# MoE slots of two expert pairs laid out by token block, one full-row scatter per two pairs, slot gates summed by one-column matmuls

## The chip, the cores and the metric

The kernel runs on one core of one Trainium2 chip. The metric is the device time of one execution in microseconds (us). PE is TensorE's matmul side, PEld its weight loads, DVE is VectorE, ACT is ScalarE, POOL is GpSimd, and SP is the engine whose queue issues the weight transfers. A line number such as L894 is a line of the kernel before. In the profile an fp32 matmul counts as two instructions (two passes), each with its own weight load; so 16 `mm` calls of the code are 32 matmuls of the trace.

## The reference

A trunk of two layers over 256 tokens of width 1024. Each layer has a token mixer (dilated attention in layer 0, a gated MLP in layer 1) and then a mixture of experts; every sub-layer is normed, modulated by a conditioning vector (adaLN) and added to x with a gate `gt`. The change touches the mixture of experts alone:

```python
def hierarchical_moe(h, w_group, b_group, w_expert, b_expert, w_gate, w_up, w_down):
    ...
    # gate: (256 tokens, 16 experts), two experts of one group of four are not zero for a token
    hg = jnp.einsum('td,edf->tef', ht, w_gate)     # 1024 -> 256
    hu = jnp.einsum('td,edf->tef', ht, w_up)
    act = (jax.nn.silu(hg) * hu * gate[..., None]).astype(h.dtype)
    y = jnp.einsum('tef,efd->td', act, w_down)     # 256 -> 1024
    return y.reshape(B, S, D)
    ...
        x = x + (gt_f[:, None, :] * y).astype(x.dtype)
```

## The kernel before, in words

The program is `attention()`, `experts(0)`, `gating()`, `experts(1)`. Each engine runs its instructions in the order in which the code writes them (the schedule is written by hand); DMAs are issued from SP's queue in that order as well. Buffers come from pools: 18 of 1 MB for weights and large tiles (`big`), 8 of half a MB (`mid`), 8 small ones, and in PSUM four single banks (`bank`) and two double ones, which hold the output sums `y[0]` and `y[1]` of the two token blocks of 128 tokens.

In `experts(l)` the router picks two experts for each token and ranks the tokens of each expert inside each block. Each expert has 32 slots (`CAP`) per block, 64 (`SL`) in all. `sel` is the one-hot matrix of tokens to slots. `gather` (L878) multiplies it with the high and low parts of the normed x and leaves the slots' inputs, transposed, in `xeT`; the first half of the experts is gathered ahead of the loop, the second half in pairs 0 to 3.

The loop runs over eight pairs p of two experts. On PE one pair is, in order:

- gate-up (L894): for eight chunks of the 1024 inputs and two experts, 64 slots as columns of PE by 512 weights (256 gate, 256 up) into the bank `pgu`. The two experts are two tiles of 64 columns side by side;
- the branch `extra(p)` (L949 to L977): an overflow pass for slots beyond the 64, which runs for one pair of this input, in layer 1, pair 4;
- two transposes `pst` in `slots` (L900) for the next pair. Their input is the one-hot times the gate (`weigh`, on POOL). ACT copies the result with a running sum, which gives each slot's gate `gs`, and DVE compares it with 0, which gives the one-hot `ST` of slots to tokens;
- in pairs 0 to 3 a piece of `gather`;
- scatter (L945) of the previous pair's result into block 0: `y[0]` gets `ST` times the high part `yhi` and times the low part `ylo`, two halves of 512 columns each, so four matmuls;
- two transposes `pat` (L916) of the activation silu(gate) x up x gs, which ACT (L909) and DVE (L910) make; DVE copies them to `atT` (L918);
- scatter of the previous pair into block 1, four matmuls more;
- down (L927): two halves of 512 outputs, each two chunks by two experts, into the bank `pd`. Then DVE multiplies with `gt` (`yw`, L931), ACT takes the high part (`yhi`, L933) and DVE the low one (`ylo`, L935).

The slots of a pair are 128 rows: expert by block by 32. Half of the rows of `ST` belong to the other block in each scatter. The last pair's result is scattered behind the loop (L1051 to L1054); there the second half of 512 columns goes as one fp32 matmul of `yw` and is not split. Behind it follow layer 1's `gating()` or the final norm and `store`. The sums `y` also take x itself, by identity matmuls (`fill`, L785).

## Time and profile before

| | |
|---|---|
| time, median of 3 runs | 616.01 us (615.84 to 616.3) |
| the profiled execution | 615.77 us, its span 614.0 us |
| PE busy | 570.5 us (93%) |
| weight loads (PEld) | 353.9 us (58%) |
| DVE busy | 346.6 us (56%) |
| ACT busy | 211.9 us (35%) |
| POOL busy | 17.7 us (3%) |
| DMA | 321 GB/s mean, 195.08 MB read |

How to read it: PE is busy in 93% of the span, and the loads run beside the matmuls. That is a mean over stages; what ends the waits in the expert loops is read from the order of time on PE in those loops. The views in order of time have these columns: start in us, duration in us, engine, line, operation, out<-in, tile, shapes and types, count, and in brackets the idle time before it and what ended it. Layer 0's expert loop runs from about 178 to 295 us of the span, layer 1's from 473 to about 597.

### The profile page before, as it was taken

What the parts mean: (1) busy time and instruction counts of PE and PEld (TensorE: products, weight loads), DVE (VectorE), ACT (ScalarE), POOL (GpSimd) and SP (SyncE); (2) the same over time, 40 slices, a digit from 0 to 9 for tenths busy, and PEclk for the clock granted to TensorE, in tenths of its full rate; (3) what the DMA queues carried; (4) which work ended last, traced back from release to release, by engine and by line L of the source; (5) the groups of instructions that cost most, each with busy time, mean ns of one, the idle gap of its engine ahead of it and who ended that gap; (6) DMA issues with size and microseconds to landing.
All of it is one profiled execution on the core that took longest, in us unless ns stands there. A gap on an engine that the chain in (4) does not pass through costs nothing. (4 is left out here: it accounts for less than half of the span.)

```text
span 614.0 us, 8150 instructions
## 1 busy us (share of the span) xinstructions
PE 570.5 (93%) x3010; PEld 353.9 (58%) x3010; DVE 346.6 (56%) x668; ACT 211.9 (35%) x357; POOL 17.7 (3%) x56
## 2 busy tenths in 40 slices
PE   6998999999988999999899989999998999989994
PEld 4766874566443444344577789998875344453341
DVE  3998876452742333232789999899457333323223
ACT  6334345551432211111543754454435111112112
POOL 1000000000010000000000010000001000000000
PEclk9999999999997999999999999999999999999998
DMA  8999869999845899999999638678832799946911
GB/s 330 423 418 420 352 257 375 417 368 420 344 184 214 331 421 420 418 415 421 418 422 395 277 140 294 250 304 350 318 138 86 301 392 416 416 176 251 414 60 68
DMA packets 29188, 197.01 MB, mean 321 GB/s; under 512 B 3328, under 2 KB 3968, under 8 KB 7616
## 3 DMA queue, kind: packets, MB, share of 16 engines
q1 hardware_dynamic: 28832, 195.61, 79.8%
q8 instruction: 38, 0.62, 0.4%
q10 hardware_dynamic: 288, 0.52, 0.2%
q14 instruction: 30, 0.25, 0.1%
HBM read 195.08 MB, written 1.05 MB: 319 GB/s over the span
## 5 line engine op out<-in xcount | busy, mean ns | idle before, releaser
L894 PE MATMUL pgu<-wgu,xeT 128*64 128x512 f32 x512 | 112.7, 592 | 0.0
L894 PEld LDWEIGHTS pgu<-wgu,xeT 128*64 128x64 f32 x512 | 36.6, 137 | 72.3 <-issue 72.0
L219 DVE SCALAR_TENSOR_TENSOR wada<-wada,cact 128x1024 f32<-128x1024 f32 x56 | 66.1, 1217 | 0.7 <-ACT cact L168 0.7
L927 PE MATMUL pd<-wdn,atT 128*64 128x512 f32 x256 | 60.2, 613 | 1.7 <-DVE atT L918 1.7
L933 ACT ACTIVATE yhi<-yw 128x512 fp32r<-128x512 f32 x32 | 20.1, 629 | 94.5 <-DVE yw L931 94.5
L910 DVE SCALAR_TENSOR_TENSOR silu<-pgu,gs,silu 128x256 f32<-128x256 f32 x16 | 7.7, 484 | 75.5 <-ACT silu L909 75.5
L931 DVE TENSOR_TENSOR yw<-pd,gt 128x512 f32<-128x512 f32 x32 | 22.0, 688 | 41.4 <-PE pd L927 41.4
L714 PE MATMUL pu<-hhi,wlo 128*128 128x256 f32 x128 | 37.0, 289 | 2.3 <-DVE wlo L296 2.3
L927 PEld LDWEIGHTS pd<-wdn,atT 128*64 128x64 f32 x256 | 17.4, 140 | 36.1 <-issue 29.1
L714 PE MATMUL pu<-hhi,whi 128*128 128x256 f32 x128 | 37.9, 296 | 0.0
L714 PE MATMUL pu<-hlo,whi 128*128 128x256 f32 x128 | 36.9, 288 | 0.0
L935 DVE TENSOR_TENSOR ylo<-yw,yhi 128x512 fp32r<-128x512 f32 x30 | 20.8, 692 | 21.5 <-ACT yhi L933 13.9
L909 ACT ACTIVATE silu<-pgu 128x256 f32<-128x256 f32 x16 | 6.1, 384 | 74.4 <-PE pgu L894 72.4
L296 DVE TENSOR_TENSOR wlo<-win,whi 128x1024 fp32r<-128x1024 f32 x25 | 30.1, 1219 | 0.6 <-ACT whi L295 0.5
L714 PEld LDWEIGHTS pu<-hhi,wlo 128*128 128x128 f32 x128 | 25.2, 197 | 2.6 <-DVE wlo L296 2.5
L286 ACT ACTIVATE hhi<-hj,B 128x256 fp32r<-128x256 f32 x16 | 8.1, 509 | 53.2 <-DVE hj L280 26.9
L295 ACT ACTIVATE whi<-win 128x1024 fp32r<-128x1024 f32 x25 | 25.7, 1052 | 1.1 <-PE pu L714 1.1
L714 PEld LDWEIGHTS pu<-hlo,whi 128*128 128x128 f32 x128 | 25.3, 198 | 0.0
L714 PEld LDWEIGHTS pu<-hhi,whi 128*128 128x128 f32 x128 | 25.2, 197 | 0.0
L296 DVE TENSOR_TENSOR wlo<-bwo,whi 128x1024 fp32r<-128x1024 f32 x16 | 19.4, 1220 | 7.8 <-ACT whi L295 6.5
L945 PE MATMUL y<-yhi,ST 128*128 128x512 f32 x60 | 21.4, 430 | 0.6 <-PEq L951 0.3
L201 PE MATMUL pada<-wada,cz 128*32 128x512 f32 x160 | 20.7, 603 | 1.3 <-ACT VV L512 1.3
(262 smaller groups left out, 1058.5 us busy)
## 6 DMA issues: line engine op xcount, KB each, us to landing
wgu<-e_gu SPq DMA_DIRECT2D x64, 1024.0 KB, 9.7
wada<-w_ada SPq DMA_DIRECT2D x48, 1024.0 KB, 11.4
wdn<-e_dn SPq DMA_DIRECT2D x32, 1024.0 KB, 10.1
win<-w_in SPq DMA_DIRECT2D x16, 1024.0 KB, 13.3
bwo<-b_wo SPq DMA_DIRECT2D x8, 1024.0 KB, 5.0
wqk<-w_qk SPq DMA_DIRECT2D x8, 960.0 KB, 19.3
wv<-w_v SPq DMA_DIRECT2D x4, 960.0 KB, 19.5
wo<-w_o SPq DMA_DIRECT2D x3, 1024.0 KB, 7.3
```

The source lines that it names most:

```text
L201: mm(acc[l][q * 32:(q + 1) * 32, :], cz[:, k, e:e + 32], w[:, q * 512:(q + 1) * 512], start=(i == i0), stop=(i == i1), skip_group_check=True)
L219: V.scalar_tensor_tensor(w[:, h * D:(h + 1) * D], w[:, h * D:(h + 1) * D], 1.0, cact, op0=OP.mult, op1=OP.mult, accum_out=modc[l][:, c:c + 1])
L286: S.activation(hx[0][:, j, :], t, AF.Identity, bias=bb[:, j:j + 1])
L295: S.activation(hi[:m, :n], w, AF.Copy)
L296: V.tensor_tensor(lo[:m, :n], w, hi[:m, :n].bitcast(F32), op=OP.subtract)
L714: mm(pu[f // 2][:, f % 2, :], w_[:, k * 512 + f * P:k * 512 + (f + 1) * P], x_[:, kc, :], start=(kc == 0 and u == 0 and f % 2 == 0), stop= ...
L894: mm(t[e * SL:(e + 1) * SL, 0:n], x(k, e), WTS[l, p][e, k // 4][:, c:c + n], start=(k == 0), stop=(k == 7), skip_group_check=True)
L927: mm(t[e * SL:(e + 1) * SL, :], at[:, f, e * SL:(e + 1) * SL], WTS[l, p][2, e][:, f, n * 512:(n + 1) * 512], start=(f == 0), stop=(f == 1) ...
L931: V.tensor_tensor(w[:, sl], t, gt[l, 1][:, sl], op=OP.mult)
L933: S.activation(hi[:, sl], w[:, sl], AF.Copy)
L935: V.tensor_tensor(lo[:, sl], w[:, sl], hi[:, sl].bitcast(F32), op=OP.subtract)
L945: mm(y[b][:, n * 512:(n + 1) * 512], st[:, b * P:(b + 1) * P], Y[xi][:, n * 512:(n + 1) * 512], start=(first and xi == 0), stop=(last and ...
```

## The change

Two pairs now form a group r. The slots of pair 2r and 2r+1 are laid out by token block: the 128 rows of one operand are four experts by 32 slots of block 0, those of the other four experts by 32 slots of block 1. Half of each comes from the one pair and half from the other, so that the results of both pairs together make full rows for one scatter per block.

- `gate_up_pair` and `down_pair` replace gate-up and down: the same columns in all, but in four tiles of 32 columns (two experts by two blocks) in place of two tiles of 64, with twice as many instructions.
- The scatter runs once per group and block: in pair 2 for both blocks, in pairs 4 and 6 for block 0 and in pairs 5 and 7 for block 1, with the last group behind the loop as before. In pairs 4 to 7 it stands ahead of `pat`.
- `group` replaces `slots`: two transposes for two pairs, ahead of the loop and in pairs 1, 3 and 5. The slots' gates are summed by four fp32 matmuls of one column with a column of ones (`onef`); DVE copies the sums (`gs2`) out, and ACT's copy with a sum goes.
- ACT's high parts and DVE's low parts are cut into two halves of 64 rows, since the two blocks go to different buffers; in the last pair the second product is cut too, and its order on DVE changes.
- `ada(A_E[l][p])` goes; it issued nothing, since the table `A_E` is all zeros.
- `extra` uses X[0], X[1] and one shared buffer `yx` in place of four buffers of the pool.

The diff, cut:

```diff
+    onef = const.tile([P, 1], F32, name="onef")
+    G.memset(onef, 1.0)
     zeros = const.tile([P, 1], BF16, name="zeros")
     G.memset(zeros, 0.0)
-    sg = [const.tile([P, NB, 2, SL], F32, name=f"sg{i}") for i in range(2)]
-    for t in sg:
-        G.memset(t, 0.0)
+    sg = [const.tile([P, NB, 4, CAP], F32, name=f"sg{i}") for i in range(2)]
...
-        def weigh(p):
-            t = sg[p % 2]
-            es = slice(2 * p, 2 * p + 2)
-            for b in range(NB):
-                G.tensor_tensor(t[:, b, :, b * CAP:(b + 1) * CAP], sel[:, b, es, :].bitcast(F32),
-                                gf[:, b, es, None].to_broadcast([P, 2, CAP]), op=OP.mult)
+        def weigh(r):
+            t = sg[r % 2]
+            for b, i, e, n in ((0, 0, 4 * r, 4), (1, 2, 4 * r, 2), (1, 0, 4 * r + 2, 2)):
+                G.tensor_tensor(t[:, b, i:i + n, :], sel[:, b, e:e + n, :].bitcast(F32),
+                                gf[:, b, e:e + n, None].to_broadcast([P, n, CAP]), op=OP.mult)
...
+        def group(src):
+            t = bank("pst", (P, T + 2))
+            for b in range(NB):
+                nc.tensor.transpose(t[:, b * P:(b + 1) * P], src[:, b].rearrange("p e c -> p (e c)"), ident)
+            for o in range(2):
+                for h in range(2):
+                    mm(t[h * SL:(h + 1) * SL, T + o:T + o + 1],
+                       src[:, h ^ o, 2 * h:2 * h + 2, :].rearrange("p e c -> p (e c)"), onef, start=True, stop=True,
+                       skip_group_check=True)
+            st = small("ST", dt=F32R)
+            V.tensor_scalar(st, t[:, 0:T], 0.0, None, op0=OP.is_gt)
+            gs = sm.tile([P, 2], F32, name="gs2", bufs=3)
+            V.tensor_copy(gs, t[:, T:T + 2])
+            return [gs[:, o:o + 1] for o in range(2)], st
+
+        def gate_up_pair(p, t):
+            for k in range(DC):
+                for q in range(4):
+                    e, b = q % 2, (q // 2) ^ (p % 2)
+                    c = (k % 4) * 512
+                    mm(t[q * CAP:(q + 1) * CAP, :],
+                       xeT[p // 4, k // 4][:, k % 4, 2 * (p % 4) + e, b * CAP:(b + 1) * CAP],
+                       WTS[l, p][e, k // 4][:, c:c + 512], start=(k == 0), stop=(k == 7), skip_group_check=True)
+
+        def down_pair(p, at, Y):
+            w = mid("yw") if p < 6 else Y[2]
+            for n in range(2):
+                t = bank("pd")
+                for f in range(2):
+                    for q in range(4):
+                        mm(t[q * CAP:(q + 1) * CAP, :], at[:, f, q * CAP:(q + 1) * CAP],
+                           WTS[l, p][2, q % 2][:, f, n * 512:(n + 1) * 512], start=(f == 0), stop=(f == 1),
+                           skip_group_check=True)
+                sl = slice(n * 512, (n + 1) * 512)
+                if p < 6 or n == 0:
+                    V.tensor_tensor(w[:, 0:512] if p > 5 else w[:, sl], t, gt[l, 1][:, sl], op=OP.mult)
+                for h in range(2):
+                    rs_, b = slice(h * SL, (h + 1) * SL), h ^ (p % 2)
+                    if p > 5 and n:
+                        V.tensor_tensor(Y[3][rs_, b, :], t[rs_, :], gt[l, 1][rs_, sl], op=OP.mult)
+                        continue
+                    S.activation(Y[0][b][rs_, sl], w[rs_, sl], AF.Copy)
+                    V.tensor_tensor(Y[1][b][rs_, sl], w[rs_, sl], Y[0][b][rs_, sl].bitcast(F32), op=OP.subtract)
+
+        def outputs(p):
+            if p < 6:
+                return [[mid(n, dt=F32R) for b in range(NB)] for n in ("yhi", "ylo")]
+            hi, lo, w = mid("yhi", (P, NB, 512), F32R), mid("ylo", (P, NB, 512), F32R), mid("yw", (P, NB, 512))
+            return [[hi[:, b, :] for b in range(NB)], [lo[:, b, :] for b in range(NB)], mid("yw0", (P, 512)), w]
+
...
-        def down(p, at, ts=(None, None), Y=None, last=False):
-            hi, lo, w = Y or (mid("yhi", dt=F32R), mid("ylo", dt=F32R), mid("yw"))
-            for n in range(2):
-                t = bank("pd") if ts[n] is None else ts[n]
-                for f in range(2):
-                    for e in range(2):
-                        mm(t[e * SL:(e + 1) * SL, :], at[:, f, e * SL:(e + 1) * SL],
-                           WTS[l, p][2, e][:, f, n * 512:(n + 1) * 512], start=(f == 0), stop=(f == 1),
-                           skip_group_check=True)
-                sl = slice(n * 512, (n + 1) * 512)
-                V.tensor_tensor(w[:, sl], t, gt[l, 1][:, sl], op=OP.mult)
-                if not last or n == 0:
-                    S.activation(hi[:, sl], w[:, sl], AF.Copy)
-                if not last:
-                    V.tensor_tensor(lo[:, sl], w[:, sl], hi[:, sl].bitcast(F32), op=OP.subtract)
-            if last:
-                sl = slice(0, 512)
-                V.tensor_tensor(lo[:, sl], w[:, sl], hi[:, sl].bitcast(F32), op=OP.subtract)
-            return hi, lo, w
-
-        def scatter(st, Y, first, last, bs=(0, 1), ns=(0, 1)):
+        def scatter(st, Y, bs=(0, 1), ns=(0, 1)):
             for b in bs:
                 for xi in range(2):
                     for n in ns:
                         mm(y[b][:, n * 512:(n + 1) * 512], st[:, b * P:(b + 1) * P],
-                           Y[xi][:, n * 512:(n + 1) * 512], start=(first and xi == 0),
-                           stop=(last and xi == 1), skip_group_check=True)
+                           Y[xi][b][:, n * 512:(n + 1) * 512], start=False, stop=False, skip_group_check=True)
 
...
-                    xr = mid("xr")
+                    xr = X[0]
...
-                    Y = mid("yhi", dt=F32R), mid("ylo", dt=F32R), mid("yw")
-                    xe = Y[2].rearrange("p (d s) -> p d s", d=DC)
+                    w = X[1]
+                    xe = w.rearrange("p (d s) -> p d s", d=DC)
...
+                    yx = mid("yx", (P, 2, 512), F32R)
+                    for n in range(2):
+                        sl = slice(n * 512, (n + 1) * 512)
+                        V.tensor_tensor(w[:, sl], tx[2 * n], gt[l, 1][:, sl], op=OP.mult)
+                        S.activation(yx[:, 0, :], w[:, sl], AF.Copy)
+                        V.tensor_tensor(yx[:, 1, :], w[:, sl], yx[:, 0, :].bitcast(F32), op=OP.subtract)
+                        for b in range(NB):
+                            for i in range(2):
+                                mm(y[b][:, sl], st[:, b * P:(b + 1) * P], yx[:, i, :], start=False, stop=False,
+                                   skip_group_check=True)
...
-        nxt = slots(weigh(0))
-        sgn = weigh(1)
+        grp = {0: group(weigh(0))}
         ada(A_B[l][3])
-        prev = None
+        Y = {}
         for p in range(8):
-            gs_, st = nxt
+            r = p // 2
             pgu[p] = bank("pgu")
-            gate_up(p, [pgu[p]], lambda k, e: xeT[p // 4, k // 4][:, k % 4, 2 * (p % 4) + e, :])
+            gate_up_pair(p, pgu[p])
...
-            act = activate(pgu[p][:, 0:T], pgu[p][:, T:2 * T], gs_)
-            if p + 1 < 8:
-                nxt = slots(sgn)
-                if p + 2 < 8:
-                    sgn = weigh(p + 2)
+            act = activate(pgu[p][:, 0:T], pgu[p][:, T:2 * T], grp[r][0][p % 2])
+            if r < 3:
+                if p % 2:
+                    grp[r + 1] = group(sgn)
+                else:
+                    sgn = weigh(r + 1)
             if p < 4:
                 gather(1, 2 * p, 2 * p + 2)
-            ada(A_E[l][p])
-            if prev:
-                scatter(*prev, False, False, (0,))
+            if p == 2 or p > 3:
+                scatter(grp[r - 1][1], Y[r - 1], (p % 2,))
             at = turn(act)
-            if prev:
-                scatter(*prev, False, False, (1,))
-            prev = (st, down(p, at, last=p == 7))
+            if p == 2:
+                scatter(grp[r - 1][1], Y[r - 1], (1,))
+            if p % 2 == 0:
+                Y[r] = outputs(p)
+            down_pair(p, at, Y[r])
...
-        st, Y = prev
+        st, Y = grp[3][1], Y[3]
         for b in range(NB):
             s = st[:, b * P:(b + 1) * P]
-            mm(y[b][:, 0:512], s, Y[0][:, 0:512], start=False, stop=False, skip_group_check=True)
-            mm(y[b][:, 512:D], s.bitcast(F32), Y[2][:, 512:D], start=False, stop=True,
-               skip_group_check=True)
-            mm(y[b][:, 0:512], s, Y[1][:, 0:512], start=False, stop=True, skip_group_check=True)
+            mm(y[b][:, 0:512], s, Y[0][b], start=False, stop=False, skip_group_check=True)
+            mm(y[b][:, 512:D], s.bitcast(F32), Y[3][:, b, :], start=False, stop=True, skip_group_check=True)
+            mm(y[b][:, 0:512], s, Y[1][b], start=False, stop=True, skip_group_check=True)
```

The order on PE in layer 0, pair 4, behind the branch of the overflow pass; `pst` are slot transposes, `y_1409` and `y_1410` the sums of token blocks 0 and 1, `pat` the transposed activations, `pd` down. Before:

```order
L900 MATMUL pst_2602<-cst_80,sg1_99 128x128 x2
L945 MATMUL y_1409<-yhi_2416,ST_2166 128x512 x2
L945 MATMUL y_1409<-ylo_2417,ST_2166 128x512 x2
L916 MATMUL pat_2615<-cst_80,silu_2599 128x128 x2
L945 MATMUL y_1410<-yhi_2416,ST_2166 128x512 x2
L945 MATMUL y_1410<-ylo_2417,ST_2166 128x512 x2
```

After:

```order
L974 MATMUL y_1409<-yhi_2244,ST_1985 128x512 x2
L974 MATMUL y_1409<-ylo_2246,ST_1985 128x512 x2
L965 MATMUL pat_2701<-cst_80,silu_2691 128x128 x2
L936 MATMUL pd_2711<-wdn_2310,atT_2704 32x512
L936 MATMUL pd_2711<-wdn_2312,atT_2704 32x512
```

The slot transposes and the scatter behind `pat` are gone; down, now in tiles of 32 columns, follows `pat` directly.

The order on PE in layer 0, pair 5, at the same place. Before:

```order
L900 MATMUL pst_2810<-cst_80,sg0_98 128x128 x2
L945 MATMUL y_1409<-yhi_2624,ST_2387 128x512 x2
L945 MATMUL y_1409<-ylo_2625,ST_2387 128x512 x2
L916 MATMUL pat_2823<-cst_80,silu_2807 128x128 x2
L945 MATMUL y_1410<-yhi_2624,ST_2387 128x512 x2
L945 MATMUL y_1410<-ylo_2625,ST_2387 128x512 x2
```

After:

```order
L909 MATMUL pst_2919<-cst_80,sg1_101 128x128 x2
L912 MATMUL pst_2919<-onef_96,sg1_101 64x1 x4
L974 MATMUL y_1410<-yhi_2245,ST_1985 128x512 x2
L974 MATMUL y_1410<-ylo_2247,ST_1985 128x512 x2
L965 MATMUL pat_2934<-cst_80,silu_2916 128x128 x2
L936 MATMUL pd_2940<-wdn_2547,atT_2937 32x512
```

The four one-column matmuls have come in behind the slot transposes, block 1's scatter has moved ahead of `pat`, and block 0's is not in this pair.

The order on DVE at the end of layer 0's loop; `yw` and `yw0` are products of down with the gate, `ylo` low parts, and `wlo` is the first weight split of the next stage. Before:

```order
L918 COPY atT_3211<-pat_3208 128x256
L931 TENSOR_TENSOR yw_3219<-pd_3220,gt_1569 128x512
L931 TENSOR_TENSOR yw_3219<-pd_3227,gt_1569 128x512
L938 TENSOR_TENSOR ylo_3218<-yw_3219,yhi_3217 128x512
L296 TENSOR_TENSOR wlo_3239<-win_3234,whi_3238 128x1024
```

After:

```order
L967 COPY atT_3353<-pat_3350 128x256
L941 TENSOR_TENSOR yw0_3152<-pd_3355,gt_1588 128x512
L948 TENSOR_TENSOR ylo_3150<-yw0_3152,yhi_3149 64x512 x2
L945 TENSOR_TENSOR yw_3151<-pd_3369,gt_1588 64x512 x2
L296 TENSOR_TENSOR wlo_3385<-win_3380,whi_3384 128x1024
```

The second product has moved behind the low parts, and both are cut in two.

## Rows read from the trace of the kernel before

**Rows 1.** PE in order of time, layer 0, pair 4; columns above, with the profile.

```profile
240.95 7.04 PE L894 MATMUL pgu<-wgu,xeT 128*64 128x512 f32 x32
248.30 0.41 PE L900 MATMUL pst<-cst,sg 128*128 128x128 f32 x2 [0.31 <-PEq L951]
248.46 0.71 PE L945 MATMUL y<-yhi,ST 128*128 128x512 f32 x2
...
249.48 0.38 PE L916 MATMUL pat<-cst,silu 128*128 128x128 f32 x2
...
250.72 3.65 PE L927 MATMUL pd<-wdn,atT 128*64 128x512 f32 x16
```

**Rows 2.** What ended the idle time before L894, whole run (us, times).

```profile
  DMA wdn<-e_dn: 0.3, 1
```

**Rows 3.** PE in order of time, layer 1, pairs 0 and 1.

```profile
473.03 0.41 PE L900 MATMUL pst<-cst,sg 128*128 128x128 f32 x2
...
481.96 0.38 PE L916 MATMUL pat<-cst,silu 128*128 128x128 f32 x2
483.30 3.65 PE L927 MATMUL pd<-wdn,atT 128*64 128x512 f32 x16 [0.96 <-DVE atT L918]
...
495.33 0.63 PE L945 MATMUL y<-yhi,ST 128*128 128x512 f32 x2
...
496.26 0.38 PE L916 MATMUL pat<-cst,silu 128*128 128x128 f32 x2
```

**Rows 4.** PE in order of time, layer 0: router, adaLN matmuls, pair 0.

```profile
164.94 2.78 PE L201 MATMUL pada<-wada,cz 128*32 128x512 f32 x24
167.72 0.21 PE L817 MATMUL pr<-a,tri 128*128 128x16 bf16 x2
...
185.18 1.06 PE L213 MATMUL pcol<-cst,arow 128*128 128x4 f32 x8
...
192.95 5.37 PE L927 MATMUL pd<-wdn,atT 128*64 128x512 f32 x16 [0.69 <-DVE atT L918]
```

**Rows 5.** PE in order of time, the overflow pass in layer 1, pair 4.

```profile
541.22 7.13 PE L894 MATMUL px<-wgu,yw 128*64 128x256 f32 x64 [0.38 <-ACT yw L988]
549.00 0.44 PE L916 MATMUL px<-cst,silu 128*128 128x128 f32 x2 [0.66 <-DVE silu L910]
549.95 3.65 PE L927 MATMUL px<-wdn,atT 128*64 128x512 f32 x16 [0.52 <-DVE atT L918]
```

**Rows 6.** PE in order of time, last pair and end of layer 0.

```profile
280.96 7.04 PE L894 MATMUL pgu<-wgu,xeT 128*64 128x512 f32 x32
288.15 0.70 PE L945 MATMUL y<-yhi,ST 128*128 128x512 f32 x2 [0.16 <-PEq L951]
...
294.87 1.12 PE L1052 MATMUL y<-yw,ST 128*128 128x512 f32 x2 [0.38 <-DVE yw L931]
```

**Rows 7.** Weight loads in order of time, start of layer 1's first gate-up.

```profile
473.36 0.20 PEld L894 LDWEIGHTS pgu<-wgu,xeT 128*64 128x64 f32 x4 [0.17 <-issue]
```

**Rows 8.** Costliest groups of the page: busy us, mean ns of one, idle before.

```profile
L894 PEld LDWEIGHTS pgu<-wgu,xeT 128*64 128x64 f32 x512 | 36.6, 137 | 72.3 <-issue 72.0
```

**Rows 9.** DVE groups by form: busy us, mean ns of one, idle before.

```profile
L296 DVE TENSOR_TENSOR wlo<-wo,whi 64x1024 fp32r<-64x1024 f32 x1 | 1.2, 1218 | 4.6 <-ACT whi L295 4.6
```

**Rows 10.** DVE in order of time, end of layer 0.

```profile
292.38 0.69 DVE L931 TENSOR_TENSOR yw<-pd,gt 128x512 f32<-128x512 f32 x1 [2.38 <-PE pd L927]
294.13 0.69 DVE L931 TENSOR_TENSOR yw<-pd,gt 128x512 f32<-128x512 f32 x1 [1.05 <-PE pd L927]
294.74 0.68 DVE L938 TENSOR_TENSOR ylo<-yw,yhi 128x512 fp32r<-128x512 f32 x1
295.33 1.22 DVE L296 TENSOR_TENSOR wlo<-win,whi 128x1024 fp32r<-128x1024 f32 x1
```

**Rows 11.** ACT in order of time, end of layer 0.

```profile
293.17 0.63 ACT L933 ACTIVATE yhi<-yw 128x512 fp32r<-128x512 f32 x1 [4.74 <-DVE yw L931]
```

**Rows 12.** Busy us and counts by stretch, PEclk, DMA share, GB/s; layer 0, pair 0.

```profile
195.00:196.00 1.00, 1.00 (x4) 0.24 (x2) 0.00 (x0) 0.00 (x0) 0.00 (x0) 0.50 1.01 426
```

More of the change, by code (lines that the diff above doesn't have):

```diff
@@ L991, in extra @@
                     gate_up(p, (tx[2], tx[0]), lambda k, e: xe[:, k, e * SL:(e + 1) * SL])
-                    Y = down(p, turn(activate(tx[2][:, 0:T], tx[0][:, 0:T], gs_), tx[1]), (tx[0], tx[2]), Y)
+                    at = turn(activate(tx[2][:, 0:T], tx[0][:, 0:T], gs_), tx[1])
                     for n in range(2):
-                        scatter(st, Y, False, False, ns=(n,))
+                        t = tx[2 * n]
+                        for f in range(2):
+                            for e in range(2):
+                                mm(t[e * SL:(e + 1) * SL, :], at[:, f, e * SL:(e + 1) * SL],
+                                   WTS[l, p][2, e][:, f, n * 512:(n + 1) * 512], start=(f == 0), stop=(f == 1),
+                                   skip_group_check=True)
[8 more added lines that the diff above has]
+                                mm(y[b][:, sl], st[:, b * P:(b + 1) * P], yx[:, i, :], start=False, stop=False,
+                                   skip_group_check=True)
         weights(l, 0, 0)
```

## The prediction

> **What bounds the kernel now.** I read the order of time on TensorE (PE) first, then what it waited for. In a middle pair of layer 0 [rows 1] the reader is to see that PE goes from one instruction group to the next: gate-up 7.04 us, 0.31 idle at the branch for the overflow pass, two slot transposes (`pst`), four scatter matmuls of token block 0, two transposes of the activations (`pat`), four scatter matmuls of block 1, then down (`pd`). Weights are no limit: over all gate-up matmuls of the run, waiting for a weight transfer cost PE 0.3 us, once [rows 2]. So the expert stages are bound by PE's own queue, in order, and what matters is not how much PE work goes but whether it covered a wait. Pair 0 of layer 1 [rows 3] shows that: it has no scatter, and down starts 1.34 us after `pat` (481.96 to 483.30), 0.96 of it idle on the DVE copy `atT`; with a half scatter in between [rows 1] the same stretch is 1.24 (249.48 to 250.72). Four matmuls there cost nothing.
>
> **The change part by part.** All in us; minus is a gain. The sum is made against the profiled execution, 615.77, which is 0.24 under the median of the three runs, 616.01.
>
> Gate-up and down with four 32-column tiles in place of two of 64. The adaLN matmuls are of the new form, four 32-column tiles with four moving operands: 24 in 2.78 [rows 4], six sets of four, 0.46 a set. Today's gate-up is 16 sets of two in 7.04 [rows 1], 0.44 a set, and down eight in 3.65 [rows 3], 0.46. A set of four takes a set of two's time, so I take **0**; how the doubled number of instructions could spoil that is a rival.
>
> Scatter. Each layer had 14 halves of four matmuls in pairs 1 to 7 (beside the last pair's six, which stay); six remain, two in pair 2 and one each in pairs 4 to 7. In pairs 1 and 3 both halves go. The one ahead of `pat` was 0.93 (495.33 to 496.26, [rows 3]) and nothing waits instead, since the gather covers the activation as in pair 0. The one behind was cover: 1.24 becomes 1.34. That is -0.83 a pair. In pairs 4 to 7 the half behind goes, and no gather eviction stands ahead of `atT` on DVE. The overflow pass has that very sequence: `pat` at 549.00, down at 549.95 [rows 5]. Its two transposes took 0.44 and not 0.38 [rows 3], so I take 0.89; 1.24 less 0.89 is -0.35 a pair. The half ahead of `pat` stays and covers the silu as today. Sum: 2 x 0.83 + 4 x 0.35 = **-3.06** a layer.
>
> Slot transposes. They stood in pairs 0 to 6 and now stand in 1, 3 and 5: 0.16 of PE each (248.30 to 248.46, [rows 1]). In pairs 4 and 6 the wait behind the branch shrinks too, as in the last pair, which has no slots: 7.19 from gate-up's start to the scatter [rows 6] against 7.35 to the transposes [rows 1]. Pairs 0 and 2 keep that wait, because the gather now has the several semaphores. Sum 4 x 0.16 + 2 x 0.16 = **-0.96** a layer, but in layer 0 pair 0 waits for ACT and DVE anyway (down there starts after 0.69 idle on `atT`, [rows 4]): over both layers -3.06 x 2 - 0.96 x 2 + 0.16 = **-7.9**.
>
> ACT's sum of the slot gates goes at no gain: it ran beside PE. Its replacement is on PE's path: four fp32 matmuls of one column, eight passes with eight loads, four times a layer (once ahead of the loop, then in pairs 1, 3, 5 between `pst` and the gather or scatter). No row has this form. Entering 64-column tiles from the transposes costs 0.17: gate-up's first loads start 0.33 behind `pst` (473.03, [rows 3], to 473.36, [rows 7]) where the scatter starts after 0.16 [rows 1]. Leaving them waits for the last matmul: the adaLN set ends at 167.72, and there the full-width `pr` starts [rows 4]. A small matmul is some 0.25 long (eight `pcol` in 1.06; at an even pace that leaves 0.12 each for the others). Between, the eight loads. From above: `pcol`'s pace, 0.17 + 1.06 = 1.23 a group. From below: loads to two column halves overlap, four of 137 ns [rows 8] within 0.20 [rows 7], so eight within some 0.15 of spread, and 0.17 + 0.15 + 0.25 is 0.55 rounded. It is not below nothing, since the two mode changes are seen. I take 0.6, near the lower end, because the row of the loads has the same two halves and `pcol` has not. Ahead of the loop gate-up follows, and the entry is paid already: 0.15 to 1.06, I take 0.3. Per layer 3 x 0.6 + 0.3 = 2.1, **+4.2** in all (3.6 to 9.5).
>
> End of the loop. For the last pair each 512-column part is cut in two row halves on ACT and DVE, and the DVE queue now has product, low part, low part, half product, half product; before, the second product came second. A half-height DVE instruction is no shorter: 64 x 1024 took 1218 ns [rows 9], 128 x 1024 1.22 us [rows 10]. So with the first product at s (292.38, [rows 10]): ACT's high part at s + 0.79 (293.17) for 0.63 [rows 11], its second half from s + 1.42, DVE's second low part from s + 2.08, then the two half products 0.61 apart (294.13 to 294.74, [rows 10]) at s + 2.69 and s + 3.30. The fp32 scatter started 0.74 behind its product's start (294.13 [rows 10] to 294.87 [rows 6]): now s + 4.04, before s + 2.49. That is +1.55 at each layer's end, with nothing beside it: **+3.1**. In other pairs the extra ACT and DVE halves, two such rounds of 2.7, end under the next gate-up of 7.04.
>
> [...]
>
> The overflow pass (run once, layer 1) now shares one buffer for high and low parts, so its second ACT copy waits for the first scatter: 0 to 0.63, the length of one such copy [rows 11]; I take **+0.2**. POOL's gate products are off the path, and no DMA is added or moved: weights are issued at the same places of SP's queue.
>
> Sum: -7.9 + 4.2 + 3.1 + 0.2 = **-0.4**; 615.77 becomes 615.4, on the median's scale **615.6**.
>
> **The rivals.** *Dear column sums* (slower): the eight passes go one behind the other at `pcol`'s pace. From 0.73 a group on (5.8 in all) the kernel is slower by 1.2; at the upper end -7.9 + 9.5 + 3.1 + 0.2 = +4.9, 620.9. For it: each group changes the tiling twice. Against: loads to two halves overlap [rows 7, 8]. Chance 0.12.
>
> *The scatter's time is all gain*: 16 halves at 1.02 [rows 1] are 16.3; with the transposes 1.9 and the costs 7.5, -10.7, 605.3. For it, PE is otherwise all but filled; against it, the uncovered 1.34 [rows 3]. Chance 0.05.
>
> *Issue pace* (slower): four narrow tiles need 64 matmuls and 64 loads where 32 of each stood. The longest dense run seen is the overflow pass, 64 in 7.13 [rows 5], 0.111 each; if that was its limit, gate-up takes 7.13 and not 7.04 and down half of that more, 0.14 x 16 = +2.2, 617.8. Against: adaLN's 24 show no such limit [rows 4]. Chance 0.06. [...]
>
> *The clock.* [...] Chances 0.10 and 0.04, and 0.04 for shifts that do not show.
>
> That the change leaves the scatter as it was can be excluded: the order of the changed program has the fewer rows.
>
> **How the numbers follow.** The sum as worked: 0.59, of which 0.37 within 0.2% (1.2 us, about what a measurement of this kernel can tell from no change), 0.18 below, since its cheap end is -7.9 + 3.6 + 2.8 + 0 = -1.5, and 0.04 above. With the rivals: faster 0.18 + 0.05 + 0.10 = 0.33; same 0.37 + 0.04 = 0.41; slower 0.04 + 0.12 + 0.06 + 0.04 = 0.26. The range: down to the cheap end with most of the clock's gain, 613.0; up to most of the dear sums, 619.8. Outside stay the all-gain case and the ends of two others.
>
> **What would show it.** Right: gate-up 7.0 to 7.1 and down 3.6 to 3.7 with twice the matmuls; `pat` to down 0.9 in pairs 4 to 7 and 1.3 in pairs 1 and 3, ended by `atT`; 0.7 to 0.8 from the slot transposes to the next full-width matmul; the last fp32 scatter idle for some 1.9 on DVE. Wrong: gate-up over 7.2; more than 1 us for a group of column sums; scatter halves gone with no idle time in their place; a granted clock below 1 at a new place.

## The result

The changed kernel takes 621.9 us (median of 4 runs, 621.36 to 622.92) and the kernel before, beside it, 615.92. The ratio is 1.0102 with a 95% interval of 1.0083 to 1.012: slower, by 6 us. The forecast was no change, 615.6, with a range up to 619.8. Two executions in a slow state, of 942.56 and 1122.76 us, are left out of the times of the two later runs to which they belong. The profiled execution of the changed kernel took 621.36 with a span of 619.0.

From the page of the changed kernel (busy us, share, instructions; then the queue that carries an engine's program: packets, MB, share):

```profile
PE 557.8 (90%) x3759; PEld 340.9 (55%) x3762; DVE 366.4 (59%) x698; ACT 221.0 (36%) x351; POOL 15.8 (3%) x47
...
q8 instruction: 44, 0.72, 0.5%
```

The same queue on the page of the kernel before:

```profile
q8 instruction: 38, 0.62, 0.4%
```

PE is busy for 12.7 us less than before (557.8 for 570.5), as the removed scatters want, and the kernel is still longer. So PE waits more. The profile has 749 more matmuls, and PE's program comes in six more pieces. The time between the starts of gate-up, pair by pair, shows where (read off the order of time on PE; the last column runs to the end of the layer's last matmul or, in layer 0, to the first of the next stage):

| us | p0 | p1 | p2 | p3 | p4 | p5 | p6 | p7 |
|---|---|---|---|---|---|---|---|---|
| layer 0 before | 20.00 | 14.20 | 14.19 | 14.41 | 13.25 | 13.52 | 13.24 | 16.43 |
| layer 0 after | 17.93 | 13.85 | 14.05 | 13.84 | 12.59 | 14.16 | 13.40 | 18.68 |
| layer 1 before | 13.42 | 14.20 | 14.91 | 14.19 | 33.40 | 13.24 | 13.25 | 16.57 |
| layer 1 after | 13.20 | 16.08 | 18.43 | 13.84 | 33.53 | 13.43 | 12.58 | 18.17 |

Most pairs moved by what the prediction's sum says. Pair 0 of layer 0 did not; it is taken up with the clock, behind the experiments. Four more did not: pairs 5 and 6 of layer 0 (what 6 lost stands partly in pair 7, since the profile puts two matmuls of gate-up among the last of down) and pairs 1 and 2 of layer 1. A quiet pair first, PE in order of time in layer 0, pair 4 of the changed kernel (the counterpart of [rows 1]):

```profile
238.51 7.05 PE L926 MATMUL pgu<-wgu,xeT 128*32 128x512 f32 x64
245.74 0.69 PE L974 MATMUL y<-yhi,ST 128*128 128x512 f32 x2 [0.18 <-PEq L979]
246.28 0.63 PE L974 MATMUL y<-ylo,ST 128*128 128x512 f32 x2
246.74 0.38 PE L965 MATMUL pat<-cst,silu 128*128 128x128 f32 x2
247.64 3.64 PE L936 MATMUL pd<-wdn,atT 128*32 128x512 f32 x32 [0.52 <-DVE atT L967]
```

Gate-up takes 7.05 with 64 matmuls for 7.04 with 32, down 3.64 for 3.65, and `pat` to down is 0.90, ended by `atT`, all as forecast. Now the pairs that did not (layer 0 pairs 5 and 6, then layer 1 pairs 1 and 2, same view):

```profile
259.20 0.41 PE L909 MATMUL pst<-cst,sg 128*128 128x128 f32 x2 [1.05 <-DVE silu L959]
...
274.38 1.04 PE L936 MATMUL pd<-wdn,atT 128*32 128x512 f32 x3 [0.52 <-DVE atT L967]
276.04 3.20 PE L936 MATMUL pd<-wdn,atT 128*32 128x512 f32 x27 [0.62 <-issue]
...
493.97 0.41 PE L909 MATMUL pst<-cst,sg 128*128 128x128 f32 x2 [1.56 <-PEq L979]
...
497.09 4.50 PE L936 MATMUL pd<-wdn,atT 128*32 128x512 f32 x32 [0.59 <-DVE atT L967]
...
512.78 1.01 PE L974 MATMUL y<-yhi,ST 128*128 128x512 f32 x2 [2.80 <-issue]
513.59 1.05 PE L974 MATMUL y<-ylo,ST 128*128 128x512 f32 x2
```

The idle times are 1.05, 0.62, 1.56 and 2.80. Two are put down to "issue" (the engine waited for nothing that the profile shows); one breaks off down after three of its matmuls, where no new operand is needed; and in the first the named releaser, `silu`, does not feed slot transposes. All four come a short time behind a skipped overflow pass. In the trace's list of transfers, a 16 KB transfer of queue q8 ends 1.4 to 1.8 us ahead of each restart: 257.41 for 259.20, 274.53 for 276.04, 492.23 for 493.97, 511.36 for 512.78. The third and fourth wait are followed by work at half the clock (busy times, then PEclk, DMA share and GB/s of four stretches):

```profile
493.00:495.00 2.00, 1.03 (x13) 0.88 (x14) 0.61 (x2) 0.00 (x0) 0.00 (x0) 1.00 0.60 213
497.00:499.00 2.00, 1.91 (x12) 0.56 (x16) 0.04 (x1) 0.00 (x0) 0.00 (x0) 0.53 1.03 430
510.00:512.00 2.00, 0.00 (x0) 0.00 (x0) 0.71 (x1) 0.78 (x1) 0.00 (x0) 1.00 0.76 266
513.00:515.00 2.00, 2.00 (x7) 1.51 (x7) 0.00 (x0) 0.00 (x0) 0.00 (x0) 0.50 1.01 397
```

In the wait itself (510 to 512) the granted clock is 1.00 with PE at zero busy; it is 0.50 in the work behind it (513 to 515). So the lower clock follows the wait and makes it dearer (1.01 and 1.05 for two scatter matmuls that take 0.69 and 0.63 in the quiet pair); it does not cause it.

**The theory (F, program fetch).** PE's program arrives in pieces while it runs: in the changed kernel's trace the 44 packets of q8, 16,384 bytes each, start between 32.74 and 602.57 us. That they are PE's is read from their number, which is higher by 6 where PE's program has 1,508 instructions more. The built programs have 11,396 and 9,888 instructions for PE, 259 and 260 for each of the 44 and 38 packets and 251 for each of the 6 between them; I take 256 a piece, an estimate from these counts (44.5 and 38.6 pieces). So nearly the whole program is transferred, the 15 skipped passes of 240 instructions with it. A border is the place where one piece ends and the next begins. Skipping the overflow pass is a jump of almost one piece. The theory says that where the jump comes soon behind a border, or lands shortly ahead of one, two borders are crossed in little time and the next piece is not there. Gate-up and down have twice the instructions in the same 7.05 and 3.64 us, so the time between two borders is halved there. No trace shows when a piece is asked for; that it is not asked for long ahead is my assumption. **The rival (W)** is that the new layout itself waits: on ACT, DVE or transfers, or for the narrow tiles.

To test this, the place of each jump was counted in the built program (labels left out). Where the borders lie was set by one offset for all kernels, at 256 instructions a piece, fitted so that the waits in layer 0 pair 6 and layer 1 pair 2 of the changed kernel begin at one; it is good to some ten instructions.

### The profile page after: what moved, and what is told of

Its sections match the earlier page's. It is cut to its first block, busy times and chain, and to the rows that moved or that the text cites. A ratio compares the mean times of both kernels' runs of the same rounds, so it can differ in the third digit from the quotient of the medians.

```text
span 619.0 us, 9649 instructions
## 1 busy us (share of the span) xinstructions
PE 557.8 (90%) x3759; PEld 340.9 (55%) x3762; DVE 366.4 (59%) x698; ACT 221.0 (36%) x351; POOL 15.8 (3%) x47
## 3 DMA queue, kind: packets, MB, share of 16 engines
HBM read 195.08 MB, written 1.05 MB: 317 GB/s over the span
## 5 line engine op out<-in xcount | busy, mean ns | idle before, releaser
L926 PE MATMUL pgu<-wgu,xeT 128*32 128x512 f32 x1024 | 114.0, 592 | 0.0
L926 PEld LDWEIGHTS pgu<-wgu,xeT 128*32 128x32 f32 x1024 | 35.6, 110 | 73.4 <-issue 72.5
L936 PE MATMUL pd<-wdn,atT 128*32 128x512 f32 x512 | 60.4, 603 | 9.6 <-DVE atT L967 7.4
L947 ACT ACTIVATE yhi<-yw 64x512 fp32r<-64x512 f32 x56 | 35.2, 628 | 90.9 <-DVE yw L941 90.2
L948 DVE TENSOR_TENSOR ylo<-yw,yhi 64x512 fp32r<-64x512 f32 x56 | 38.5, 687 | 20.8 <-ACT yhi L947 20.0
L941 DVE TENSOR_TENSOR yw<-pd,gt 128x512 f32<-128x512 f32 x28 | 19.4, 692 | 37.1 <-PE pd L936 36.7
L936 PEld LDWEIGHTS pd<-wdn,atT 128*32 128x32 f32 x512 | 16.1, 111 | 43.4 <-issue 31.7
L589 PE MATMUL y<-whi,ghi 128*128 128x512 f32 x64 | 20.9, 398 | 0.0
```

Source lines behind the costliest of these rows:

```text
L589: mm(y[b][:, n * 512:(n + 1) * 512], x_[:m, c, b * P:(b + 1) * P], w_[:m, n * 512:(n + 1) * 512], start=(first and i == 0), stop=(last and ...
L926: mm(t[q * CAP:(q + 1) * CAP, :], xeT[p // 4, k // 4][:, k % 4, 2 * (p % 4) + e, b * CAP:(b + 1) * CAP], WTS[l, p][e, k // 4][:, c:c + 512 ...
L936: mm(t[q * CAP:(q + 1) * CAP, :], at[:, f, q * CAP:(q + 1) * CAP], WTS[l, p][2, q % 2][:, f, n * 512:(n + 1) * 512], start=(f == 0), stop= ...
L941: V.tensor_tensor(w[:, 0:512] if p > 5 else w[:, sl], t, gt[l, 1][:, sl], op=OP.mult)
L947: S.activation(Y[0][b][rs_, sl], w[rs_, sl], AF.Copy)
L948: V.tensor_tensor(Y[1][b][rs_, sl], w[rs_, sl], Y[0][b][rs_, sl].bitcast(F32), op=OP.subtract)
```

## The experiments

### No branch: both kernels without the overflow pass

```diff
         def extra(p):
+            return
             v = nc.values_load(nx[0:1, p:p + 1], min_val=0, max_val=3)
```

The changed kernel:

> The changed kernel with the overflow pass and its branch left out (so the slots beyond 64 of layer 1, pair 4, are missing from the output). Theory F (program fetch): the new idle times of PE in the changed kernel (1.05 in layer 0 pair 5, 0.62 in pair 6, 1.56 and 2.80 in layer 1 pairs 1 and 2, with the clock at half speed behind the last two) come because PE's program, which arrives in transfers of 16 KB, is jumped over at each skipped pass and the next piece is not there yet. Without the branch the program runs straight on, so these stalls go: the time falls by the pass itself (20.9), by some 8.7 of stalls and by up to 0.3 at each of 15 branches, to 588 to 593, and it is 0 to 4 FASTER than the kernel before without the pass. Theory W (the new layout itself: waits on ACT, DVE and transfers, or narrow tiles): the stalls stay without a branch; 596 to 601, and 4 to 7 slower than the kernel before without the pass.

The kernel before:

> The kernel before with the overflow pass and its branch left out (the same part of the output is missing). It is the partner of the run above. Both theories: 615.9 less the pass (20.6), less some 0.2 to 0.3 at each of 15 branches and less the 1.2 of small stalls behind branches: 589 to 594.

Measured: 589.89 (4 runs, 587.22 to 590.17) and 587.53 (587.29 to 589.47). The four waits are gone: from gate-up to gate-up pairs 1 and 3 take 13.47 to 13.49 (13.84 or 13.85 in the partner), pair 2 13.66 (13.86), pairs 4 and 6 12.5 (12.9), pair 5 13.07 (12.90). But the changed kernel is 2.4 slower than its partner, where the expectation by theory F was 0 to 4 faster. The difference stands mainly at two places: pair 0 of layer 0, where down took 5.01 for 3.64, and the end of layer 1, where the wait for the last products is followed by slow work (the two fp32 scatters below took 1.12 and 1.02 in the partner):

```profile
576.87 1.29 PE L1097 MATMUL y<-yw,ST 128*128 128x512 f32 x2 [1.67 <-DVE yw L945]
577.43 1.15 PE L1098 MATMUL y<-ylo,ST 128*128 128x512 f32 x1
578.39 0.63 PE L1096 MATMUL y<-yhi,ST 128*128 128x512 f32 x1
578.81 1.91 PE L1097 MATMUL y<-yw,ST 128*128 128x512 f32 x2
```

So the four waits need the branch, as theory F has it; that the layout has no cost of its own is not shown by this pair.

### The jumps moved away from the borders

```diff
+PADS = ((32, 17, 20, 17, 31, 21, 31, 10), (27, 17, 20, 17, 0, 41, 31, 0))
...
                     tx = [bank("px") for _ in range(3)]
+                    for _ in range(PADS[l][p]):
+                        mm(tx[0][0:1, 0:1], zeros, zeros, start=True, stop=True)
...
-        warm(W2)
+        warm(W2, 8)
```

> The changed kernel, with nothing changed in the work that the expert loops execute: one-element matmuls are added inside the overflow pass where it is skipped (none where it runs), and two rows of eight warm-up matmuls of 512 columns outside the expert loops are cut into 64 of 64 columns each. That makes the program longer (12,270 instructions of PE for 11,396) and moves every jump to the middle of a 16 KB piece of the program. Theory F: the stalls go, 8.7 with what follows from them, so 612 to 615, faster than the kernel before. Theory W: 621 to 623, no change.

Measured: 614.22 (5 runs, 613.22 to 614.65), ratio to the kernel before 0.9962 (0.9947 to 0.9976). The added matmuls of the pass are never executed, and the cut warm-up rows alone save nothing ("Only the place of the jumps changed", below, has them without the padding); together they made the changed kernel 7.7 us faster. Layer 1, pairs 1 and 2, the places of the waits of 1.56 and 2.80, in order of time on PE:

```profile
492.97 0.41 PE L913 MATMUL pst<-cst,sg 128*128 128x128 f32 x2 [0.32 <-PEq L983]
...
507.37 0.64 PE L881 MATMUL pg<-sel,xlo 128*128 128x256 f32 x4
507.85 0.63 PE L978 MATMUL y<-yhi,ST 128*128 128x512 f32 x2
508.31 0.62 PE L978 MATMUL y<-ylo,ST 128*128 128x512 f32 x2
```

The wait behind the branch is 0.32, and the scatter follows the gather without one. Pairs 5 of layer 0 and 1 and 2 of layer 1 take 13.43, 13.86 and 14.03. The loops execute the same work in the same layout, so theory W is out for these waits.

### The kernel before, with its jumps moved to the borders

The same edit, with counts of 66 to 116 one-element matmuls in pairs 0 to 7 (none in layer 1, pairs 4 and 7) and the warm-up left alone.

> The kernel before, with one-element matmuls added only inside the overflow pass where it is skipped, so nothing that is executed changes; the counts are chosen so that 12 of the jumps come some 10 instructions behind a 16 KB border of PE's program and two land 1 or 2 instructions ahead of one. Theory F: each such jump makes PE wait, 0.3 to 2.5 us where nothing hides it, 5 to 25 us in all: 621 to 641. Theory W: 615 to 617, no change.

Measured: 638.31 (636.07 to 640.15), 22 slower than the kernel before with every executed instruction the same. Layer 0, pair 1 in order of time on PE:

```profile
198.66 7.04 PE L896 MATMUL pgu<-wgu,xeT 128*64 128x512 f32 x32
208.01 0.41 PE L902 MATMUL pst<-cst,sg 128*128 128x128 f32 x2 [2.31 <-PEq L953]
208.18 0.79 PE L880 MATMUL pg<-sel,xhi 128*128 128x256 f32 x4
208.77 1.05 PE L880 MATMUL pg<-sel,xlo 128*128 128x256 f32 x4
209.62 1.05 PE L947 MATMUL y<-yhi,ST 128*128 128x512 f32 x2
```

The wait is 2.31 where 0.31 stood, and the scatter behind it runs at 1.05 for 0.63: the pair grew from 14.20 to 17.76. All of layer 0's pairs 1 to 7 grew, by 2 to 3.7. One thing was not as I had it: in layer 1, where by my count the jumps come 16 to 18 instructions behind a border, pairs 1 to 3 did not wait at all (14.19 to 14.20). In layer 0 it was 7 to 10. The trace's packets of q8 show the difference: in layer 0, pair 1, the packet ended at 206.29, 0.6 behind the end of gate-up, and in layer 1, pair 1, at 515.06, 2.1 ahead of it (517.18). There PE did not wait. Why so few instructions move the packet by 2.7 us stays open. The two jumps that land 1 or 2 ahead of a border (layer 1, pairs 5 and 6) cost 0.8 and 0.6.

### Only the place of the jumps changed

```diff
-        warm(W2)
+        warm(W2, 8)
```

> The changed kernel with nothing added in the overflow pass; only the two rows of eight warm-up matmuls outside the expert loops are cut into 64 narrow ones, so that PE's program is 112 instructions longer ahead of each loop and every jump stands elsewhere against the 16 KB borders. Theory F says where the idle times go, counted in the program: in layer 0 the jump of pair 2 comes 27 instructions behind a border and that of pair 3 lands 28 ahead of one; in layer 1 that of pair 1 lands 19 ahead of one. So these three pairs get longer than in the padded kernel (14.03, 13.84 and 13.86 from gate-up to gate-up), by 0.5 to 3 each; pairs 5 and 6 of layer 0 and pair 2 of layer 1, which waited in the changed kernel (14.16, 13.40 and 18.43), fall to 13.4, 12.6 and 14.05. Pairs 7 (44 behind a border, and 36 ahead of one) are at the edge, 0 to 1. In all 616 to 620. Theory W: the idle times stay where they were, pairs 5 and 6 of layer 0, 1 and 2 of layer 1, 621 to 623.

Measured: 624.52 (3 runs, 622.63 to 625.5). The expectation names the places ahead of the run, and they came out: pairs 2 and 3 of layer 0 took 15.03 and 16.57, pair 1 of layer 1 19.17; pairs 5 and 6 of layer 0 fell to 13.44 and 12.59, pair 2 of layer 1 to 14.04. The time is above my 616 to 620, because the waits reach 2.6 and the work behind them is slower (down took 5.24 and 5.42 for 3.64; the mean granted clock is 0.982, in the changed kernel 0.991). Layer 0, pair 3 and layer 1, pair 1, on PE; in the second the row of eight one-column matmuls breaks off after seven.

```profile
238.30 5.24 PE L938 MATMUL pd<-wdn,atT 128*32 128x512 f32 x32 [2.04 <-issue]
...
497.98 0.39 PE L914 MATMUL pst<-onef,sg 128*64 128x1 f32 x7
500.97 0.16 PE L914 MATMUL pst<-onef,sg 128*64 128x1 f32 x1 [2.60 <-issue]
501.09 1.20 PE L879 MATMUL pg<-sel,xhi 128*128 128x256 f32 x4
```

### What the kernel before itself loses

The cure of the second experiment on the kernel before, with counts of its own.

> The kernel before with the same cure as the padded changed kernel: one-element matmuls where the overflow pass is skipped, two rows of warm-up matmuls cut, all jumps away from the 16 KB borders. It asks what the kernel before itself loses to program fetch. Theory F: the small stalls behind branches (0.22 and 0.27 in layer 0 pairs 3 and 5, 0.45 and 0.26 in layer 1 pair 2) go: 0.5 to 1.5 less than the kernel before. Rival: these stalls are something else, no change (within 0.3).

Measured: 614.28 (12 runs), ratio 0.998 (0.9969 to 0.9991): 1.7 us by the medians, 1.2 by the ratio. Its pairs become even, in layer 0 14.19 in each of 1 to 3 and 13.24 or 13.25 in 4 to 6, and pair 2 of layer 1 falls from 14.91 to 14.24. The largest of the waits that went stood there in the kernel before:

```profile
510.02 0.39 PE L878 MATMUL pg<-sel,xlo 128*128 128x256 f32 x1 [0.45 <-issue]
```

With the jumps out of the way the two kernels cannot be told apart: 614.22 and 614.28, with ratios to the kernel before whose intervals just overlap.

### The end of the loop

```diff
-                for h in range(2):
+                for h in ((1, 0) if p == 7 else (0, 1)):
...
+                    if p == 7:
+                        low_parts.append((rs_, b))
+                        continue
                     V.tensor_tensor(Y[1][b][rs_, sl], w[rs_, sl], Y[0][b][rs_, sl].bitcast(F32), op=OP.subtract)
+            for rs_, b in low_parts:
+                V.tensor_tensor(Y[1][b][rs_, 0:512], w[rs_, 0:512], Y[0][b][rs_, 0:512].bitcast(F32), op=OP.subtract)
...
+        for b in range(NB):
+            s = st[:, b * P:(b + 1) * P]
             mm(y[b][:, 0:512], s, Y[1][b], start=False, stop=True, skip_group_check=True)
```

> The padded changed kernel (614.2) with the last pair's order on DVE turned: both half products ahead of the low parts, the half that block 0 needs first, and the low-part matmuls of both blocks last. If the end term of the prediction is right (1.55 at each layer's end because the second product stands behind the low parts), the last pair falls by 1.2 to 1.6 a layer: 611 to 612. Rival: the end of the loop is bound by the low parts, which now come later; then it moves under 0.5 a layer, 613.2 to 614.5.

Measured: 612.13 (4 runs, 610.58 to 613.27), ratio 0.9939 (0.9917 to 0.9961), so 2.1 less than the padded kernel where 2.2 to 3.2 was expected. The two layers differ: in layer 1 pair 7 fell from 18.03 to 16.27, more than expected, and in layer 0 only from 17.87 to 17.50, as the rival had it, since there DVE's own queue ends last. DVE at the end of layer 0:

```profile
291.22 1.41 DVE L950 TENSOR_TENSOR yw<-pd,gt 64x512 f32<-64x512 f32 x2 [1.05 <-PE pd L941]
292.66 1.41 DVE L958 TENSOR_TENSOR ylo<-yw,yhi 64x512 fp32r<-64x512 f32 x2
293.99 1.21 DVE L300 TENSOR_TENSOR wlo<-win,whi 128x1024 fp32r<-128x1024 f32 x1
295.12 2.47 DVE L1119 COPY X<-y 128x512 f32<-128x512 f32 x4
```

The last sums are ready on PE at some 294.6, but the copy of `y` waits for the two extra halves and for `wlo`, which belongs to the next stage.

### The slot gates summed by ACT

```diff
-                    mm(t[h * SL:(h + 1) * SL, T + o:T + o + 1],
-                       src[:, h ^ o, 2 * h:2 * h + 2, :].rearrange("p e c -> p (e c)"), onef, start=True, stop=True,
-                       skip_group_check=True)
+                    q, b = slice(h * SL, (h + 1) * SL), h ^ o
+                    S.activation(junk[q, 0:P], t[q, b * P:(b + 1) * P], AF.Copy, accum_out=gs[q, o:o + 1])
```

> The padded changed kernel with the slot gates summed by four ACT copies of 64 x 128 a group in place of the eight one-column passes on PE (pads set anew). The trace of the padded kernel has 0.67 from the slot transposes to the next full-width matmul and 0.64 to gate-up, where the kernel before has 0.16 and 0.33: 3 x 0.51 + 0.31 a layer, so 3.7 less: 610 to 611.5. Rival: the ACT copies hold the bank of the transposes and delay down, which then gives it back: 613 to 616.

Measured: 623.21 (4 runs, 622.95 to 627.19), 9 slower than the padded kernel: the rival, and dearer than it said. Pairs 1 and 3 take 16.62 to 16.65 in both layers. Layer 0, pair 1; DVE first, then PE:

```profile
205.75 0.42 DVE L920 TENSOR_SCALAR ST<-pst 128x256 fp32r<-128x256 f32 x1 [1.91 <-ACT junk L918]
206.09 0.80 DVE L889 TENSOR_SCALAR xeT<-pg,G,B 128x512 f32<-128x512 f32 x1
206.81 0.41 DVE L969 COPY atT<-pat 128x256 f32<-128x256 f32 x1
```

```profile
207.33 5.29 PE L938 MATMUL pd<-wdn,atT 128*32 128x512 f32 x32 [2.54 <-ACT xeT L887]
```

Four copies with their accumulator reads take 2.0 on ACT; DVE's one-hot `ST` waits 1.91 for them, `atT` stands behind it, and down waits 2.54 and then takes 5.29 for 3.64. So the one-column matmuls, at half a us a group, are better than these copies as they stand; with `ST` written ahead of the copies it was not run.

### All edits together, twice

First with ACT's sums, the turned end, and a gather that is cut in two around the activation transposes (padding counts set anew):

```diff
             for xi, b, x_ in ((0, 0, xhi), (0, 1, xhi), (1, 0, xlo), (1, 1, xlo)):
+                if xi and not b and between:
+                    at = between()
...
-                gather(1, 2 * p, 2 * p + 2)
+                at = gather(1, 2 * p, 2 * p + 2, (lambda: turn(act)) if p != 2 else None)
```

> The padded changed kernel with both edits above and one more: in pairs 0, 1 and 3 the activation transposes go between the gather's high and low halves, so that four gather matmuls cover the wait for the copy of the transposes (0.90 to 0.96 idle ahead of down in these pairs). Sum if all three are additive: 3.0 + 3.7 + 6 x 0.7 to 0.9, so 602 to 604. Rival: the transposes then wait for the activation, or down for a bank that the gather's eviction holds; 606 to 609.

Measured: 614.17 (9 runs, 611.41 to 615.95), outside both expected ranges. ACT's sums spoil it (pairs 1 and 3 at 14.22 or 14.23, with 1.80 of wait ahead of down), but pair 0 of layer 1, which has none, fell from 13.20 to 12.53. So the sums went back to PE, and the next stage's first weight split went ahead of the last pair's products:

```diff
+            if p == 7 and l == 0:
+                in_load(0)
+                ada_load(1)
+                in_split(0, 0)
             down_pair(p, at, Y[r])
-        if l == 0:
-            in_load(0)
-            ada_load(1)
-            in_split(0, 0)
```

> The padded changed kernel with the turned order of the last pair, the slot gates summed on PE as in the change, and two more edits: in pairs 0, 1 and 3 the activation transposes go between the gather's high and low halves, and at the end of layer 0 the next stage's first weight split (1.04 on ACT, 1.21 on DVE) stands ahead of the last pair's products, in DVE's wait for down, in place of behind them. From the traces: 612.1 with the turned order; pair 0 of layer 1 fell by 0.67 with the split gather, so six times that is 4.0; the split ahead frees DVE for layer 0's sums 1.2 earlier: 606 to 608. Rival: gather's evictions hold the banks of down in pairs 1 and 3, where a slot transpose stands ahead, so those pairs gain nothing: 609 to 611.

Measured: 608.92 (6 runs, 608.12 to 610.71), ratio to the kernel before 0.9901 (0.9884 to 0.9918). It beats both kernels, by 7 and by 13 us, and ends 0.9 above the 606 to 608 that was expected: pair 4 of layer 1 took 34.54 for 33.23 in the padded kernel, with the granted clock at 0.57 in 549 to 553, behind the overflow pass, where two scatter matmuls took 0.98 and 1.06 and down 4.08 for 3.64. Pair 7 of layer 0 fell from 17.50 to 16.84. Layer 0, pair 1 on PE:

```profile
205.13 0.38 PE L978 MATMUL pat<-cst,silu 128*128 128x128 f32 x2
205.26 0.72 PE L883 MATMUL pg<-sel,xlo 128*128 128x256 f32 x4
206.03 3.64 PE L944 MATMUL pd<-wdn,atT 128*32 128x512 f32 x32
```

`pat` to down is 0.90 where it was 1.28 in the changed kernel, with four gather matmuls inside; pairs 1 and 3 take 12.98 or 12.99.

## Why the prediction was wrong

**The step that failed** is the first of the part by part: gate-up and down with twice the instructions at "0". For the execution of the instructions it held (7.05 and 3.64). But a program of 1,508 more PE instructions has its borders elsewhere and passes them faster, and the prediction had no term for that. The rival on the number of instructions looked at issue pace alone; queue q8 with its 38 packets of 16 KB stood on the page of the kernel before and was not read. The forecast gave 0.26 to slower, but none of the causes that it named for it brought the loss: gate-up kept its pace, a group of column sums cost 0.51, and the lower clock, one of its signs of being wrong, came at new places only behind two of the waits. The price, against the padded kernel pair by pair: 0.73 in layer 0 pair 5, 1.62 in pairs 6 and 7 (13.40 + 18.68 against 12.59 + 17.87), 2.22 and 4.40 in layer 1 pairs 1 and 2: 9.0, the slow clock behind the waits included. By the medians it is 7.7 (621.9 to 614.2). The spans of the two profiled executions differ by 6.8, since pair 0 of layer 0 ran 2.7 faster in the changed kernel's profile than in the padded one's (17.93 and 20.64). The kernel before loses 1.2 by its pairs and by the ratio, at the same kind of place: the waits of 0.2 to 0.5 that stood in its trace.

**The rest of the sum held.** The two padded kernels are free of these waits and show its terms one by one:

| term, us a pair or place | forecast | padded kernels |
|---|---|---|
| pairs 1 and 3 (scatter out, column sums in) | -0.83 + 0.6 = -0.23 | 14.19 to 13.84: -0.35 |
| pair 2 (no slot transposes) | -0.16 | 14.19 to 14.03: -0.16 |
| pairs 4 and 6 | -0.35 - 0.32 = -0.67 | 13.25 to 12.59: -0.66 |
| pair 5 | -0.35 + 0.6 = +0.25 | 13.25 to 13.43: +0.18 |
| pair 7 and end | -0.35 + 1.55 = +1.2 | 16.45 to 17.87: +1.42 (layer 0) |
| a layer's first sums | +0.3 | 0.64 for 0.31 to gate-up: +0.33 |
| whole kernel | -0.4 | 614.28 to 614.22: -0.1 (by the two ratios -1.1) |

- Scatter: right. In the changed kernel `pat` to down is 0.90 in pairs 4 to 7 and 1.28 in pairs 1 and 3, ended by `atT`. That a scatter behind `pat` was cover and not cost is what kept its removal from being a gain, and the cut gather shows it from the other side: four matmuls put there cost nothing.
- Column sums: 0.67 from the transposes to the next full-width matmul, less 0.16, is 0.51 for the 0.6 that I took.
- End of the loop: the first fp32 scatter waited 1.67 (1.9 forecast) and came at s + 4.24, not s + 4.04. In DVE's queue the half products start 0.70 apart, 293.37 and 294.07, and the kernel before's two last instructions 0.61 apart [rows 10]. So they start 0.09 further apart than I took; why is not shown. The first product, the half products and that scatter in the changed kernel, layer 0:

```profile
290.58 0.69 DVE L941 TENSOR_TENSOR yw<-pd,gt 128x512 f32<-128x512 f32 x1 [2.05 <-PE pd L936]
293.37 1.39 DVE L945 TENSOR_TENSOR yw<-pd,gt 64x512 f32<-64x512 f32 x2
294.82 1.13 PE L1096 MATMUL y<-yw,ST 128*128 128x512 f32 x2 [1.67 <-DVE yw L945]
```

- Clock: pair 0 of layer 0 is a case of its own. It took 20.00 before, 17.93 after, 20.64 in the padded changed kernel and 18.27 in the padded kernel before; its down ran in 5.37 [rows 4], 3.64, 6.17 and 3.65, with a granted clock of 0.50 before [rows 12], 1.00 after and 0.50 in the padded changed kernel (193.5 to 196 in both). So both speeds come in both layouts, and the 2 us that the changed kernel's profile gains there cannot be put down to the change; what decides it was not found. The clock's gain, which the forecast's range counts in its low end of 613.0, is thus a term that no run shows: the runs had both clocks there, whatever the layout.

## What to carry to other kernels

A branch over a block that is nearly always skipped made the place of every later instruction matter here: 7.7 us between the changed kernel and its padded copy, 22 between the kernel before and its copy with the jumps at the borders. Before splitting wide matmuls into more narrow ones, count the engine's instructions, divide by the packets of its program queue, and look for waits that end shortly behind one of them; padding inside the skipped block moved the borders at no cost in executed work (614.22 with it). When matmuls are removed, ask first which wait they stood in: of the eight scatter halves that went in a layer, six stood behind `pat` and were cover for the most part (`pat` to down is 1.24 with one in [rows 1]; without it 0.90, and 1.28 in pairs 1 and 3).

## What the runs showed of the hardware that I had not expected

- A late piece of the program cost up to 2.8 us of PE, and 2.2 to 5.3 a pair where slower work followed it (layer 1: 2.22 and 4.40 in pairs 1 and 2 of the changed kernel, 5.31 in pair 1 of the run in which only the place of the jumps changed). It shows as "issue" (2.80) or under the name of a releaser that has nothing to do with the instruction (`silu`, 1.05), once in the middle of a row of equal matmuls (2.60, behind the seventh of eight).
- The price differs with the place. In layer 1's pair 7 of the changed kernel the jump comes 12 instructions behind a border, and PE did not wait for it (18.17 against 18.03 in the padded kernel): its packet ended at 597.84, 2.4 ahead of the end of gate-up, and the weight transfers were over by then (DMA share 0.00 from 593 to 596, 0.02 from 595 to 598). In pairs 1 and 2 of that layer the DMA share was 0.6 to 1.0. That weight transfers delay the pieces is possible and not tested; they do not decide it alone, since in the kernel before with its jumps at the borders the piece came in time in layer 1, pair 1, at a DMA share of 0.99 (511 to 515).
- Eight one-column fp32 matmuls in 64-column tiles take 0.33 with the change of tiling behind them (204.51 to 204.84 in layer 0, pair 1 of the changed kernel), less than half of the 1.06 that eight of `pcol`'s kind take.
